# Sums of weight blocks in a seven-product FFN stage: additions on GpSimd replaced by accumulating SBUF-to-SBUF transfers in place, with the minus signs moved to the sums of x^T

## The chip, the cores and the metric

The kernel runs on one core of a Trainium2 chip. The metric is the device time of one execution in microseconds (us), as the median of several runs. The core has a matrix engine (TensorE, PE in the profile, with PEld for its weight loads), VectorE (DVE), ScalarE (ACT), GpSimd (POOL) and a sync engine (SP). Each of them works through its own queue of instructions in order. 16 DMA engines move data; transfers are issued here by SP (all weight loads) and by POOL.

## The reference, cut to what matters

The layer has two feed-forward networks, one at each end, with a recurrent branch and an attention branch between them. Only the two networks are touched by the change:

```
def swiglu(x, w1, w3, w2):
    return (jax.nn.silu(x @ w1) * (x @ w3)) @ w2
...
f = swiglu(rms_norm(h, ffn1_pre_g[l]), ffn1_w1[l], ffn1_w3[l], ffn1_w2[l])
...
f = swiglu(rms_norm(h, ffn2_pre_g[l]), ffn2_w1[l], ffn2_w3[l], ffn2_w2[l])
```

x is 512 x 1024, w1 and w3 are 1024 x 2816, all in float32. The other inputs do not matter here.

## The kernel before

**Arithmetic.** Every float32 operand of TensorE is split in two fp32r parts: `hi` is a copy of the source on ACT (it rounds), `lo` is the source minus `hi` on DVE (`split2`, lines 190 and 191). A product takes three matmuls: hi x hi, lo x hi, hi x lo.

**Units.** The first column tiles of w1 and w3 are worked one by one. A unit is a product of one 128-column tile of the weights with all of x: 24 matmuls of 512 columns (`mm_feat`, lines 200 to 202). `get` (line 159 on) loads the raw tile (`raw_...`, 512 KB, by SP, line 140) and splits it two units ahead (lines 155 and 156). There are six such tiles of w1 and of w3 in the first network (`NC1 = 6`) and four in the second (`NC2 = 4`).

**Pairs.** The remaining tiles are worked two at a time (`class Pairs`): 16 jobs in the first network, 18 in the second. A job takes two raw tiles, `ra` and `rb`, whose halves are the four blocks a11, a12 (of `ra`) and a21, a22 (of `rb`), and multiplies them with the four quarters of x^T by a scheme with seven products instead of eight. For it, sums of weight blocks (s1 to s4) and sums of the quarters of x^T (t1 to t4, function `sums`) are needed. One product is 12 matmuls of 256 columns (`mm_s`, lines 451 to 453). In job n the products stand on PE in this order: a11, s1, then a22 of the job before (`last`), then s2, a12, s4, s3. The product s2 adds onto the PSUM bank of a11, so it also waits until ACT has copied that bank out (`q1`, line 528).

**Preparation of a job.** `prep(m, i)` prepares job m in five steps. Step 0 makes the four sums with four additions of 128x512 (lines 496 to 499) into two slots of their own; POOL does them, except for the very first job, where DVE does. Steps 1 to 4 split `ra`, the slot of s1 and s2, the slot of s3 and s4, and a22. In job n, step 0 of job n+2 and steps 1 to 4 of job n+1 are issued, and `raws(n + 3)` issues the two loads of job n+3. Before the first job there are no products of pairs to hang the steps on, so they are put at points between the last units with `later`; a point comes twice in a unit, and the n-th point counts from where `later` is called. The first network has 8 units there, so `end` is 16 points.

**Slots.** All tiles of this size share 42 slots of SBUF (`NSLOT`). An instruction that writes a slot first waits until the last use of its former tile is over. This holds for SP's loads, too.

**Other work near the start.** A table of attention biases, `bias_scr`, is written to DRAM by one large transfer that POOL issues (line 672).

Of the kernel before, what the change touches and what calls it, by code (L numbers as in the profile page):

```python
# [12 lines left out]
AF = mybir.ActivationFunctionType  # L13
ALU = mybir.AluOpType

P = 128
# [35 lines left out]
def hybrid_layer(ctx: ExitStack, tc: tile.TileContext, a: dict, out: bass.AP):  # L52
    nc = tc.nc
    act, dve, pool, pe, sp = nc.scalar, nc.vector, nc.gpsimd, nc.tensor, nc.sync
# [77 lines left out]
    raws, pairs = {}, {}  # L132
# [41 lines left out]
    def later(n, fn, rank=1):  # L174
        uid[0] += 1
        due.append((now[0] + n, rank, uid[0], fn))
# [11 lines left out]
    def split2(hi, lo, src):  # L188

        act.activation(hi, src, AF.Copy)  # L190
        dve.tensor_tensor(out=lo, in0=src, in1=f32(hi), op=ALU.subtract)  # L191
# [247 lines left out]

    QH = 4 * P

    def mm_s(wa, x, ps, more=False):
# [11 lines left out]
    class Pairs:  # L456
# [13 lines left out]
        def prep(self, m, i, eng=None):  # L470
            if m >= len(self.jobs) or (m, i) in self.ready:
                return
            self.ready.add((m, i))
            k = self.k0 + 2 * m
            if i == 0:
                if k not in loaded or k + 1 not in loaded:
                    self.raws(m)
                s12, s34 = slot([P, 2 * QH], name="S12"), slot([P, 2 * QH], name="S34")
                self.w[m] = {"r": (raws.pop(k), raws.pop(k + 1)), "s": (s12, s34)}
            W = self.w[m]  # L480
            (ra, rb), (s12, s34) = W["r"], W["s"]
            a11, a12, a21, a22 = ra[:, :QH], ra[:, QH:], rb[:, :QH], rb[:, QH:]

            def both(src, w=2 * QH):
                hi = slot([P, w], F32R, name="whi")
                lo = slot([P, w], F32R, name="wlo")
                split2(hi, lo, src)
                return hi, lo

            def halves(p, a, b):  # L490
                W[a] = p[0][:, :QH], p[1][:, :QH]
                W[b] = p[0][:, QH:], p[1][:, QH:]

            if i == 0:
                e = eng or pool
                e.tensor_tensor(out=s12[:, :QH], in0=a21, in1=a22, op=ALU.add)
                e.tensor_tensor(out=s12[:, QH:], in0=s12[:, :QH], in1=a11, op=ALU.subtract)
                e.tensor_tensor(out=s34[:, QH:], in0=a12, in1=s12[:, QH:], op=ALU.subtract)
                e.tensor_tensor(out=s34[:, :QH], in0=a11, in1=a21, op=ALU.subtract)
            elif i == 1:  # L500
                halves(both(ra), "a11", "a12")
            elif i == 2:
                halves(both(s12), "s1", "s2")
            elif i == 3:
                halves(both(s34), "s3", "s4")
            elif i == 4:
                t = slot([P, 2, QH], F32R, name="w22")
                split2(t[:, 0, :], t[:, 1, :], a22)
                W["a22"] = t[:, 0, :], t[:, 1, :]
                del W["r"], W["s"]  # L510

        def run(self, tail, hooks={}):
            X = self.X
            assert st["get"] == st["split"] == self.k0, (st, self.k0)
            st["get"] = st["split"] = self.k0 + 2 * len(self.jobs)
            last = lambda: None
            for n, (nm, f) in enumerate(self.jobs):
                W = self.w.pop(n)
                first = nm == self.na
                tmp = slot([P, 4, 256], name="ct")  # L520
                q1, q5, u, v = (tmp[:, i, :] for i in range(4))
                c = slot([P, 2, SEQ], name="cc")
                if first:
                    self.c1[f] = c
                bu, bx, bc = (bank("c")[:, :256] for _ in range(3))
                at = lambda i: [f() for f in hooks.get((n, i), ())]
                mm_s(W["a11"], X["b11"], bu)
                act.activation(q1, bu, AF.Copy)
                at(1)
                mm_s(W["s1"], X["t1"], bx)  # L530
                act.activation(q5, bx, AF.Copy)
                at(2)
                last()
                self.prep(n + 1, 1)
                mm_s(W["s2"], X["t2"], bu, True)
                del W["s1"], W["s2"]
                act.activation(u, bu, AF.Copy)
                at(3)
                if n == len(self.jobs) - 1:
                    tail()  # L540
                self.prep(n + 1, 2)

                def c11():
                    mm_s(W["a12"], X["b21"], bc)
                    del W["a11"], W["a12"]
                    dve.tensor_tensor(out=c[:, 0, :256], in0=bc, in1=q1, op=ALU.add)

                if n < len(self.jobs) - 1:
                    c11()
                mm_s(W["s4"], X["b22"], bx, True)  # L550
                dve.tensor_tensor(out=c[:, 0, 256:], in0=bx, in1=u, op=ALU.add)
                self.prep(n + 1, 3)
                mm_s(W["s3"], X["t3"], bu, True)
                del W["s3"], W["s4"]
                act.activation(v, bu, AF.Copy)
                dve.tensor_tensor(out=c[:, 1, 256:], in0=v, in1=q5, op=ALU.add)
                if n == len(self.jobs) - 1:
                    c11()
                if not first:
                    c1 = self.c1[f]  # L560
                    dve.tensor_tensor(out=c1[:, 0, :], in0=c1[:, 0, :], in1=c[:, 0, :], op=ALU.mult)
                    dve.tensor_tensor(out=c1[:, 1, 256:], in0=c1[:, 1, 256:], in1=c[:, 1, 256:], op=ALU.mult)
                self.prep(n + 1, 4)
                self.prep(n + 2, 0)
                self.raws(n + 3)

                def last(W=W, bu=bu, c=c, f=f, first=first):
                    mm_s(W.pop("a22"), X["t4"], bu, True)
                    if first:
                        act.activation(c[:, 1, :256], bu, AF.Silu)  # L570
                        act.activation(c[:, 0, :], c[:, 0, :], AF.Silu)
                        act.activation(c[:, 1, 256:], c[:, 1, 256:], AF.Silu)
                    else:
                        c1 = self.c1.pop(f)
                        dve.tensor_tensor(out=c1[:, 1, :256], in0=bu, in1=c1[:, 1, :256], op=ALU.mult)
                        self.hid.f += [c1[:, 0, :], c1[:, 1, :]]

            last()


# [40 lines left out]
    pairs_a = Pairs("w1a", "w3a", NC1, X1, hid)  # L621
# [32 lines left out]
    s4 = small(NT, "s4")  # L654
# [4 lines left out]
    r = rstd_of(s4, during=lambda q: act.activation(tiny, q, AF.Silu))  # L659
# [15 lines left out]
    for t in range(NT):  # L675
        pe.matmul(psr[:, t * P : (t + 1) * P], ones, dgs[:, t, :], start=True, stop=True)
    act.activation(Rb, psr, AF.Copy)
    pairs_a.prep(0, 1)
    hid.f += [silu_mul(ps[0], ps[1], Rb), silu_mul(ps[2], ps[3], Rb)]
    pairs_a.prep(0, 2)  # L680
    later(1, lambda: pairs_a.prep(0, 3))
    later(2, lambda: pairs_a.prep(0, 4))

# [34 lines left out]
    def sums(xf):  # L718

        t = [slot([P, 4, 256], name="T") for _ in range(4)]  # L720
        pool.tensor_tensor(out=t[2], in0=xf[1, 1], in1=xf[0, 1], op=ALU.subtract)
        dve.tensor_tensor(out=t[0], in0=xf[0, 1], in1=xf[0, 0], op=ALU.subtract)
        dve.tensor_tensor(out=t[1], in0=xf[1, 1], in1=t[0], op=ALU.subtract)
        dve.tensor_tensor(out=t[3], in0=xf[1, 0], in1=t[1], op=ALU.subtract)
        return t

    def to_slots(src):
# [24 lines left out]
    later(9, lambda: X1.update(t1=to_slots(tn[0])))  # L752
    later(11, lambda: X1.update(t2=to_slots(tn[1])))
    end = 2 * 2 * (NC1 - 2)
    for i, at_ in enumerate((end - 5, end - 2, end - 1)):
        later(at_, lambda i=i: pairs_a.prep(1, i))
    swiglu_units("w1a", "w3a", 2, NC1, hid, Rb)
    point(True)
# [152 lines left out]
    for t in range(NT):  # L911
        ps = bank("v")
        c = slice(t * P, (t + 1) * P)
        o = ps[:, :256]
        for k in range(KT):
            wh, wl = wv[k // 4]
            s = slice((k % 4) * 256, (k % 4 + 1) * 256)
# [191 lines left out]
    xf = {(hh, th): slot([P, 4, 256], name="xf") for hh in range(2) for th in range(2)}  # L1109
# [10 lines left out]
        later(2 + i, lambda i=i: X2.update({f"t{i + 1}": to_slots(tn[i])}))  # L1120
    pairs_b = Pairs("w1b", "w3b", NC2, X2, hid)
    end = 2 * 2 * (NC2 - 2)
    for i, at_ in enumerate((end - 7, end - 4, end - 3, end - 2, end - 1)):
        later(at_, lambda i=i: pairs_b.prep(0, i))
    later(end, lambda: pairs_b.prep(1, 0))
    swiglu_units("w1b", "w3b", 2, NC2, hid)
    point(True)
    X2["t4"] = to_uT(tn[3], 0, 1)
# [75 lines left out]
```

## Time and profile before

| what | us |
|---|---|
| median of 3 runs | 1140.14 (1140.09 to 1140.4) |
| the profiled execution | 1140.29 |
| its span in the trace | 1138.5 |
| jobs of the first network, from 74 to 235 of the span | 161 |
| jobs of the second network, from 830 to 1012 of the span | 182 |
| POOL busy in these two stretches | 106.31 and 107.96 |
| an addition of 128x512 on POOL | 1.29 to 2.28 |
| an addition of 128x512 on DVE (lines 496 to 499) | 0.68 to 0.69 |
| a `lo` of 128x1024 on DVE, beside POOL's additions | mean 1.66 (`wlo<-S`), up to 2.31 |
| the same with POOL idle | 1.22 |

The profile gives time by engine and by line, by stretch of the span, as a chain of waits that ends with the last instruction, and as a list of instructions in order of time. "Busy" of PE counts pipelined matmuls, so that it says whether PE ever stood still, and not how near it is to its peak. Starts of instructions are in us from the start of the span.

### The profile page before, as it was taken

The numbers are of one execution on the slowest core, as the hardware profiler recorded it, in microseconds if no ns is written. First come the engines' busy times: TensorE is split into PE (matmuls) and PEld (weight loads), VectorE is DVE, ScalarE is ACT, GpSimd is POOL, SyncE is SP. The second block draws the span as 40 slices with busy tenths as digits, with TensorE's granted clock in tenths as the row PEclk, the third lists the DMA queues.
The fourth block names the chain that finished last, engine by engine and source line by source line (L and its number), as shares of the span: only waits on it lengthen the run. The fifth ranks groups of instructions, "written<-read, shape, count | busy, mean of one in ns | idle before, by whom it ended". The sixth has DMA issues, their size and how long they took to land.

```text
span 1138.5 us, 17073 instructions
## 1 busy us (share of the span) xinstructions
PE 1129.9 (99%) x6691; PEld 1006.8 (88%) x6691; DVE 778.5 (68%) x1180; ACT 572.0 (50%) x1021; POOL 341.8 (30%) x259
## 2 busy tenths in 40 slices
PE   9999999999999999999999999999999999999997
PEld 7889999988889888888888888889899999998886
DVE  5997889885447746684678864667968678985313
ACT  7445555564325357844656662356445555574211
POOL 0148677500001000001555640000655567700000
PEclk9999999999999999999999999999999999999999
DMA  9943323265314311234122333532133332255101
GB/s 339 155 138 112 100 88 111 87 210 166 98 57 152 120 56 56 90 97 130 56 78 90 93 99 105 170 126 93 37 94 112 112 98 89 93 189 180 39 19 55
DMA packets 36800, 124.93 MB, mean 110 GB/s; under 512 B 4400, under 2 KB 5936, under 8 KB 36720
## 3 DMA queue, kind: packets, MB, share of 16 engines
q1 hardware_dynamic: 34128, 115.15, 30.6%
q0 software_dynamic: 2448, 8.43, 3.9%
q8 instruction: 52, 0.85, 0.3%
q10 hardware_dynamic: 144, 0.26, 0.1%
q14 instruction: 28, 0.23, 0.1%
HBM read 116.50 MB, written 7.33 MB: 109 GB/s over the span
## 4 chain that ended last, share of the span: by engine, by line
PE 94%; DMA 4%; DVE 1%; SPq 0%; ACT 0%; issue 0%; DVEq 0%; ACTq 0%
PE f L201 11%; PE f L202 11%; PE f L200 11%; PE c L453 10%; PE c L452 10%; PE c L451 10%; PE acc L219 8%; PE acc L218 8%; PE acc L220 8%; DMA raw_w1a<-in_w1a_dram 2%; PE pt L1019 1%; DMA h<-in_x_dram 1%; PE s L983 1%; PE s L982 1%; PE tr L291 1%; PE o L1035 1%
## 5 line engine op out<-in xcount | busy, mean ns | idle before, releaser
L200 PE MATMUL f<-uT,whi 128*128 128x512 f32 (+1 forms) x536 | 196.1, 366 | 0.0
L201 PE MATMUL f<-uT,wlo 128*128 128x512 f32 (+1 forms) x536 | 195.2, 364 | 0.3 <-DVE wlo L156 0.3
L202 PE MATMUL f<-uT,whi 128*128 128x512 f32 (+1 forms) x536 | 195.1, 364 | 0.0
L218 PE MATMUL acc<-whi,hT 128*128 128x512 f32 x352 | 137.1, 390 | 0.0
L219 PE MATMUL acc<-wlo,hT 128*128 128x512 f32 x352 | 137.0, 389 | 0.0
L220 PE MATMUL acc<-whi,hT 128*128 128x512 f32 x352 | 136.9, 389 | 0.0
L201 PEld LDWEIGHTS f<-uT,wlo 128*128 128x128 f32 x536 | 101.2, 189 | 16.4 <-DVE wlo L156 0.7
L191 DVE TENSOR_TENSOR wlo<-S,whi 128x1024 fp32r<-128x1024 f32 x68 | 112.8, 1659 | 4.1 <-ACT whi L190 3.8
L453 PE MATMUL c<-Xl,whi 128*128 128x256 f32 x408 | 115.5, 283 | 0.0
L453 PE MATMUL c<-uT,whi 128*128 128x256 f32 x408 | 115.5, 283 | 0.0
L452 PE MATMUL c<-Xh,wlo 128*128 128x256 f32 x408 | 115.5, 283 | 0.0
L452 PE MATMUL c<-uT,wlo 128*128 128x256 f32 x408 | 115.5, 283 | 0.0
L451 PE MATMUL c<-Xh,whi 128*128 128x256 f32 x408 | 115.5, 283 | 0.0
L451 PE MATMUL c<-uT,whi 128*128 128x256 f32 x408 | 115.5, 283 | 0.0
L202 PEld LDWEIGHTS f<-uT,whi 128*128 128x128 f32 x536 | 101.1, 189 | 15.9
L200 PEld LDWEIGHTS f<-uT,whi 128*128 128x128 f32 x536 | 101.2, 189 | 15.6
L1003 POOL TENSOR_SCALAR P<-P,d 128x256 f32<-128x256 f32 (+1 forms) x64 | 63.1, 1001 | 56.0 <-DVE d L1001 33.9
L452 PEld LDWEIGHTS c<-Xh,wlo 128*128 128x128 f32 x408 | 78.3, 192 | 0.0
L452 PEld LDWEIGHTS c<-uT,wlo 128*128 128x128 f32 x408 | 78.3, 192 | 0.0
L451 PEld LDWEIGHTS c<-Xh,whi 128*128 128x128 f32 x408 | 78.3, 192 | 0.0
L451 PEld LDWEIGHTS c<-uT,whi 128*128 128x128 f32 x408 | 78.3, 192 | 0.0
L453 PEld LDWEIGHTS c<-uT,whi 128*128 128x128 f32 x408 | 78.3, 192 | 0.0
(313 smaller groups left out, 2673.7 us busy)
## 6 DMA issues: line engine op xcount, KB each, us to landing
raw_w2a<-in_w2a_dram SPq DMA_DIRECT2D x22, 512.0 KB, 4.1
raw_w1b<-in_w1b_dram SPq DMA_DIRECT2D x22, 512.0 KB, 3.9
raw_w3b<-in_w3b_dram SPq DMA_DIRECT2D x22, 512.0 KB, 3.9
raw_w2b<-in_w2b_dram SPq DMA_DIRECT2D x22, 512.0 KB, 4.2
raw_w3a<-in_w3a_dram SPq DMA_DIRECT2D x21, 512.0 KB, 4.4
raw_w1a<-in_w1a_dram SPq DMA_DIRECT2D x20, 512.0 KB, 4.3
raw_wg<-in_wg_dram SPq DMA_DIRECT2D x16, 512.0 KB, 4.0
raw_xr<-in_xr_dram SPq DMA_DIRECT2D x8, 512.0 KB, 3.9
```

Of the source, the lines that this page charges most:

```text
L191: dve.tensor_tensor(out=lo, in0=src, in1=f32(hi), op=ALU.subtract)
L200: pe.matmul(ps[:, c0:c1], wh[:, s], h_, start=k == 0, stop=False)
L201: pe.matmul(ps[:, c0:c1], wl[:, s], h_, start=False, stop=False)
L202: pe.matmul(ps[:, c0:c1], wh[:, s], l_, start=False, stop=k == KT - 1)
L218: pe.matmul(acc[n], x[:, 0, c], wh[:, s], start=first, stop=False)
L219: pe.matmul(acc[n], x[:, 0, c], wl[:, s], start=False, stop=False)
L220: pe.matmul(acc[n], x[:, 1, c], wh[:, s], start=False, stop=last)
L291: pe.transpose(ps[:, k * P : (k + 1) * P], hg[:, kk * P : (kk + 1) * P], ident)
L451: pe.matmul(ps, wh[:, s], xh, start=first, stop=False, skip_group_check=True)
L452: pe.matmul(ps, wl[:, s], xh, start=False, stop=False, skip_group_check=True)
L453: pe.matmul(ps, wh[:, s], xl, start=False, stop=k == 3, skip_group_check=True)
L1003: pool.tensor_scalar(out=pt[:, x, b0:256], in0=pt[:, x, b0:256], scalar1=d[:, x : x + 1], scalar2=None, op0=ALU.mult)
```

## The change

The sums of a job are made in place, in the raw tiles, all with a plus sign, by four additions in this order, called A1 to A4 below:

- A1: a22 += a21 (this is s1)
- A2: a21 += a11 (s3)
- A3: a11 += a22 (s2)
- A4: a12 += a11 (s4)

On the first job of the first network DVE does them, as before. On all others each is a transfer from SBUF to SBUF with addition at the destination, issued by POOL: 128 rows of 2 KB, 256 KB. Since the blocks are overwritten, a22 and `ra` have to be split before: step 0 is now the split of a22 and A1, step 1 the split of `ra` and A2 to A4, step 2 the split of `rb` (s3 and s1), step 3 the split of `ra` again (s2 and s4). In job n, steps 0 and 1 of job n+2 and steps 2 and 3 of job n+1 are issued. A1 to A4 depend on each other: A2 reads and overwrites a21 after A1 has read it, A3 adds what A1 left in a22 to the a11 that A2 has read, and A4 adds what A3 left. In the program each of A2 to A4 waits on POOL for the landing of the one before it; A1 waits for its raw tile and for the split of a22, A3 also for the split of `ra`.

Two slots per job for s1 to s4 are no longer taken. Ahead of the first job, the steps stand at other points. The signs that the sums of the weights lose are given to t1 to t4 (DVE makes all four now; one was POOL's before) and to three reads of PSUM: two copies on ACT with scale -1, an addition turned into a subtraction, and a multiplication on DVE with a scalar of -1 added. The program has the same 6,686 matmuls; POOL's additions of two tensors go from 150 to 16, and its transfers from 28 to 160.

```
             if i == 0:
                 if k not in loaded or k + 1 not in loaded:
                     self.raws(m)
-                s12, s34 = slot([P, 2 * QH], name="S12"), slot([P, 2 * QH], name="S34")
-                self.w[m] = {"r": (raws.pop(k), raws.pop(k + 1)), "s": (s12, s34)}
+                self.w[m] = {"r": (raws.pop(k), raws.pop(k + 1))}
...
+            def add(to, x):
+                if eng:
+                    eng.tensor_tensor(out=to, in0=to, in1=x, op=ALU.add)
+                else:
+                    pool.dma_start(out=to, in_=x, accum_op=ALU.add)
...
             if i == 0:
-                e = eng or pool
-                e.tensor_tensor(out=s12[:, :QH], in0=a21, in1=a22, op=ALU.add)
-                e.tensor_tensor(out=s12[:, QH:], in0=s12[:, :QH], in1=a11, op=ALU.subtract)
-                e.tensor_tensor(out=s34[:, QH:], in0=a12, in1=s12[:, QH:], op=ALU.subtract)
-                e.tensor_tensor(out=s34[:, :QH], in0=a11, in1=a21, op=ALU.subtract)
-            elif i == 1:
-                halves(both(ra), "a11", "a12")
-            elif i == 2:
-                halves(both(s12), "s1", "s2")
-            elif i == 3:
-                halves(both(s34), "s3", "s4")
-            elif i == 4:
                 t = slot([P, 2, QH], F32R, name="w22")
                 split2(t[:, 0, :], t[:, 1, :], a22)
                 W["a22"] = t[:, 0, :], t[:, 1, :]
-                del W["r"], W["s"]
+                add(a22, a21)
+            elif i == 1:
+                halves(both(ra), "a11", "a12")
+                add(a21, a11)
+                add(a11, a22)
+                add(a12, a11)
+            elif i == 2:
+                halves(both(rb), "s3", "s1")
+            elif i == 3:
+                halves(both(ra), "s2", "s4")
+                del W["r"]
...
                 act.activation(q5, bx, AF.Copy)
                 at(2)
+                self.prep(n + 2, 0)
                 last()
-                self.prep(n + 1, 1)
+                self.prep(n + 2, 1)
                 mm_s(W["s2"], X["t2"], bu, True)
...
-                self.prep(n + 1, 2)
+                self.raws(n + 3)
...
                 dve.tensor_tensor(out=c[:, 0, 256:], in0=bx, in1=u, op=ALU.add)
-                self.prep(n + 1, 3)
+                self.prep(n + 1, 2)
                 mm_s(W["s3"], X["t3"], bu, True)
                 del W["s3"], W["s4"]
-                act.activation(v, bu, AF.Copy)
-                dve.tensor_tensor(out=c[:, 1, 256:], in0=v, in1=q5, op=ALU.add)
+                act.activation(v, bu, AF.Copy, scale=-1.0)
+                dve.tensor_tensor(out=c[:, 1, 256:], in0=v, in1=q5, op=ALU.subtract)
...
-                self.prep(n + 1, 4)
-                self.prep(n + 2, 0)
-                self.raws(n + 3)
+                self.prep(n + 1, 3)
...
-    pairs_a.prep(0, 1)
+    pairs_a.prep(0, 1, dve)
     hid.f += [silu_mul(ps[0], ps[1], Rb), silu_mul(ps[2], ps[3], Rb)]
-    pairs_a.prep(0, 2)
-    later(1, lambda: pairs_a.prep(0, 3))
-    later(2, lambda: pairs_a.prep(0, 4))
+    later(1, lambda: pairs_a.prep(0, 2))
+    later(2, lambda: pairs_a.prep(0, 3))
...
-        pool.tensor_tensor(out=t[2], in0=xf[1, 1], in1=xf[0, 1], op=ALU.subtract)
-        dve.tensor_tensor(out=t[0], in0=xf[0, 1], in1=xf[0, 0], op=ALU.subtract)
-        dve.tensor_tensor(out=t[1], in0=xf[1, 1], in1=t[0], op=ALU.subtract)
-        dve.tensor_tensor(out=t[3], in0=xf[1, 0], in1=t[1], op=ALU.subtract)
+        dve.tensor_tensor(out=t[0], in0=xf[0, 0], in1=xf[0, 1], op=ALU.subtract)
+        dve.scalar_tensor_tensor(out=t[1], in0=xf[1, 1], scalar=-1.0, in1=t[0], op0=ALU.mult, op1=ALU.subtract)
+        dve.tensor_tensor(out=t[2], in0=xf[1, 1], in1=xf[0, 1], op=ALU.subtract)
+        dve.scalar_tensor_tensor(out=t[3], in0=t[1], scalar=-1.0, in1=xf[1, 0], op0=ALU.mult, op1=ALU.subtract)
...
-    for i, at_ in enumerate((end - 5, end - 2, end - 1)):
+    for i, at_ in enumerate((end - 9, end - 8, end - 2, end - 1)):
         later(at_, lambda i=i: pairs_a.prep(1, i))
...
-    for i, at_ in enumerate((end - 7, end - 4, end - 3, end - 2, end - 1)):
-        later(at_, lambda i=i: pairs_b.prep(0, i))
-    later(end, lambda: pairs_b.prep(1, 0))
+    for m, i, at_ in ((0, 0, end - 7), (0, 1, end - 6), (1, 0, end - 5), (1, 1, end - 4), (0, 2, end - 2), (0, 3, end - 1)):
+        later(at_, lambda m=m, i=i: pairs_b.prep(m, i))
```

More of the change, by code (lines that the diff above doesn't have):

```diff
@@ L477, in prep @@
                     self.raws(m)
-                s12, s34 = slot([P, 2 * QH], name="S12"), slot([P, 2 * QH], name="S34")
-                self.w[m] = {"r": (raws.pop(k), raws.pop(k + 1)), "s": (s12, s34)}
+                self.w[m] = {"r": (raws.pop(k), raws.pop(k + 1))}
             W = self.w[m]
-            (ra, rb), (s12, s34) = W["r"], W["s"]
+            ra, rb = W["r"]
             a11, a12, a21, a22 = ra[:, :QH], ra[:, QH:], rb[:, :QH], rb[:, QH:]
@@ L569, in last @@
                     if first:
-                        act.activation(c[:, 1, :256], bu, AF.Silu)
+                        act.activation(c[:, 1, :256], bu, AF.Silu, scale=-1.0)
                         act.activation(c[:, 0, :], c[:, 0, :], AF.Silu)
@@ L574, in last @@
                         c1 = self.c1.pop(f)
-                        dve.tensor_tensor(out=c1[:, 1, :256], in0=bu, in1=c1[:, 1, :256], op=ALU.mult)
+                        dve.scalar_tensor_tensor(out=c1[:, 1, :256], in0=bu, scalar=-1.0, in1=c1[:, 1, :256], op0=ALU.mult, op1=ALU.mult)
                         self.hid.f += [c1[:, 0, :], c1[:, 1, :]]
```

## The prediction

> **What bounds the kernel now.** I read the share of each engine first, then the chain of waits, then stretches of the span.
>
> ```profile
> PE 1129.9 (99%) x6691; PEld 1006.8 (88%) x6691; DVE 778.5 (68%) x1180; ACT 572.0 (50%) x1021; POOL 341.8 (30%) x259
> PE 94%; DMA 4%; DVE 1%; SPq 0%; ACT 0%; issue 0%; DVEq 0%; ACTq 0%
> 0.00:20.00 20.00, 18.55 (x71) 14.59 (x72) 12.06 (x24) 13.37 (x25) 2.04 (x9) 1.00 0.91 306
> 40.00:60.00 20.00, 19.73 (x88) 16.00 (x87) 19.83 (x30) 5.73 (x7) 2.40 (x1) 1.00 0.99 152
> 74.00:235.00 161.00, 161.00 (x1344) 161.00 (x1343) 133.81 (x138) 90.99 (x158) 106.31 (x56) 1.00 0.35 115
> 830.00:1012.00 182.00, 182.00 (x1516) 181.92 (x1515) 141.89 (x152) 99.71 (x174) 107.96 (x63) 1.00 0.33 105
> ```
>
> The last four rows are stretches: from and to, length, then busy time of PE, PEld, DVE, ACT and POOL, PE's clock, the share of the DMA engines, GB/s. In both stretches of pairs PE never stands still, at full clock: 161 us for 1,344 matmuls is 0.12 us each, whatever DVE and POOL do beside it. A product is 12 x 0.12 = 1.44 us and a job seven of them, 10.08 us (ACT's copy of `q1`, line 528, also returns every 10.08 us). PE's idle time is 1138.5 - 1129.9 = 8.6 us, most of it in the tail; before 80 us it is 1.45 + 0.27 = 1.7 us. So whatever the change frees on POOL and DVE has at most 1.7 us to win. It can only lose, if a sum comes too late.
>
> **POOL's additions removed.** 132 of them go, some 1.3 to 2.3 us each. They lay beside PE. DVE's `lo` gets shorter with them (1.66 to 1.22 us), also beside PE. Worth: 0. The scale of -1 and the fourth sum of x^T on DVE (1.22 us at 128x1024) cost about what DVE saves near the start, where POOL's sum had stretched line 414 to 1.80 us from 0.69: 0.
>
> **The chain of transfers.** A2, A3 and A4 each wait on POOL for the landing of the one before, and POOL's queue is in order, so A1 of the next job stands behind A4 of this one; only A4's landing and the next A1 overlap. If a transfer takes L from issue until a waiting instruction runs, and P is POOL's own time to issue one, jobs can leave POOL no faster than every 3L + P. POOL's transfers in the trace:
>
> ```profile
> L964 POOL DMA_DIRECT2D BT<-bias_scr x16: 536/536/590, 523.9 to 607.5; - x16
> DMA to landing us min/median/max: 2.3/2.4/4.1
> DMA to landing us min/median/max: 3.9/4.7/7.3
> 523.89 2.17 POOL L964 DMA_DIRECT2D BT<-bias_scr  x4 [164.81 <-PE f L202]
> 527.99 0.30 POOL L965 MEMSET BT<- 64x256 f32 x1 [1.92 <-DMA BT<-bias_scr]
> 528.61 2.12 POOL L964 DMA_DIRECT2D BT<-bias_scr  x4
> 533.89 0.31 POOL L965 MEMSET BT<- 64x256 f32 x1 [3.17 <-DMA BT<-bias_scr]
> ```
>
> The first two lines are BT, 128 KB each: P = 0.54, landing 2.4. The third is the loads of line 248, 512 KB each: 3.9 at best. The rest is POOL in order of time: the fourth BT transfer starts at 523.89 + 2.17 - 0.54 = 525.52 and the memset that waits for it at 527.99, so L = 2.47. In the second group, with a weight load issued at 529.07 beside it, it is 533.89 - 530.19 = 3.70: 1.2 us more.
>
> No row shows a transfer that adds. Lower bound: it costs what a copy of 256 KB would, between the two rows, 2.4 + (3.9 - 2.4) x 128/384 = 2.9. Upper bound: it reads source and destination, so it costs as 512 KB do, 3.9, plus, with SP's two loads in each job, 1.2 us on two of three transfers, 0.8 each: 4.7. Below a plain copy nothing can lie. I take the middle of 2.9 and 3.9 with one such meeting in most jobs: 3.4 + 0.3 = 3.7. POOL's period is then 3 x 3.7 + 0.54 = 11.64, 1.56 above the job's 10.08. It decides from 3L + P = 10.08, L = 3.18.
>
> The lead that hides the first jobs: A1 of job n+2 can be issued 2.88 (two products) + 0.38 (`q5`) + 0.62 + 0.68 (split of a22) = 4.6 us into job n. A4 is wanted 2.0 us into job n+2: s2 is its fourth product, at 4.32, less 1.05 + 1.22 for the split. That is 2 x 10.08 + 2.0 - 4.6 = 17.6 us for 4L = 14.8; slack 2.8. Second network, jobs 2 to 17: 15 periods x 1.56 = 23.4, less the slack 2.8, plus 1.7 because job 0's chain starts only some 17 us ahead and pushes the next two: **22**. First network, jobs 2 to 15: 13 x 1.56 = **20**, with no slack left after the start below. ACT and DVE wait in order, too: behind the late second split of `ra` stand `q1` and the split of a22 for two jobs on, but both are needed later than s2 is, so they add nothing.
>
> **The start.** Step 0 of job 1 moves from POOL at point 11 to ACT and DVE at point 7. Job 1's raw tiles aren't there then:
>
> ```profile
> 51.43 6.00 SPq L140 DMA_DIRECT2D raw_w3a<-in_w3a_dram  x2
> 51.74 1.04 ACT L190 ACTIVATE Xh<-xn 128x1024 fp32r<-128x1024 f32 x1
> 54.26 1.06 ACT L155 ACTIVATE whi<-raw_w1a 128x1024 fp32r<-128x1024 f32 x1 [1.48 <-DMA raw_w1a<-in_w1a_dram]
> 65.74 1.29 POOL L496 TENSOR_TENSOR S<-raw_w3a 128x512 f32<-128x512 f32 x1 [13.57 <-DMA raw_w3a<-in_w3a_dram]
> bias_scr<-erow POOLq DMA_DIRECT2D x1, 3064.0 KB, 33.6
> ```
>
> SP issues them at 51.43 and 57.1; POOL, which had nothing else to do, waited 13.57 us for them, until 65.74, because `bias_scr` filled the DMA engines until 29.6 + 33.6 = 63.2. In the changed program the split of a22 stands on ACT right after `Xh<-xn` (51.74), and behind it the split of `ra` and then `whi` of the seventh of eight units (54.26 now). ACT would wait there, and DVE with it. SP can issue these loads some 5 to 10 us earlier in the changed program (fewer slots are taken; the second one waits for the third unit's end, about 47), but they stand in SP's queue behind the eighth unit's tile, which landed at 32.7 + 28.2 = 60.9. So they land between 60.9 and 65.1; I take T = 63. Then a22 (0.62 on ACT), `ra` (1.05) and the unit's split (1.05 + 1.22, with DVE's hand-over) put its `lo` at T + 4 = 67, and PE wants it at 30.3 + 6 x 5.46 = 63.1 (units take 24 x 0.2275 us, the first of the eight starts at 30.3): **3.9**.
>
> The chain of job 1 starts at T + 1.4 and ends at T + 1.4 + 4L; the second split of `ra` waits for it on ACT, and behind it stand a `silu` and `q1` of job 0. With 2.3 for the split and 2.8 for those, `q1` is done at T + 4L + 6.5; s2 of job 0 wants it at T + 4 + 2 x 5.46 + 2.88 = T + 17.8. So 4L - 11.3 = **3.5** at L = 3.7.
>
> Sum: 22 + 20 + 3.9 + 3.5 = 49.4, on the span of 1138.5. The profiled execution took 1140.29, 1.8 more than its span and 0.15 more than the median, so 1138.5 + 49.4 + 1.8 = 1189.7: I say **1190**.
>
> The Trainium skill, "DMA: Bandwidth & Descriptors" (Anatomy of one DMA — SWDGE (gpsimd) path), gives about 2.0 us plus bytes/436e3 for a transfer that POOL issues, and "Collectives: The Full Stack" (The bandwidth ceiling) says that a reducing transfer is slower than a copy because it needs two source reads, not because of the add. As an estimate from the two, 2.0 + 524/436 = 3.2 alone; the BT row agrees with the first (2.3 by it, 2.4 measured); no run here shows the second. By them the period would be 10.1, next to the job's 10.08, and the sum about 1146.
>
> **The rivals.** (1) *The chain fits under a job.* A transfer from SBUF to SBUF that costs as a plain copy, L = 2.9, gives 3 x 2.9 + 0.54 = 9.24, under 10.08. For it: BT's 2.4. Against: the destination is read too, and loads take a third of the DMA engines (0.35 and 0.33 above). Left is the start, 3.9 + 0.3: 1140.3 + 4.2 = 1144.5; the skill's formula above lies at its edge. (2) *Adding is slow in itself.* If the adder passes data slower than 512 KB would go, L = 6: period 18.5, excess 8.5; 13 x 8.5 + 15 x 8.5 + 17 at the start = 255: 1395. For and against: no row. (3) *Not slower.* Job 1's raw tiles land early enough, before 63.1 - 4.0 = 59.1, and L is under 2.83, which hides both prices of the start; then only DVE's relief is left, up to 1.7 us: 1139. For it: SP's loads wait less for slots. Against: the tile ahead of them in SP's queue landed at 60.9. That the program doesn't do what it says I rule out: its list of instructions has 132 transfers in place of the additions.
>
> **How the numbers follow.** No change that a measurement of this kernel can tell is within 0.2%, 2.3 us. Chances: forecast (L 3.2 to 4.7) 0.55, rival 1 0.25, rival 2 0.10, rival 3 0.10. The forecast's own ends: L = 3.2 gives about 1147; L = 4.7 a period of 14.64, excess 4.56: 59 + 4 and 68 + 6 in the two networks, 3.9 + 7.5 at the start, 1289. The range takes in rival 1 but for its lowest part: 1143 to 1285; outside are rival 2 and most of rival 3. Faster by over 0.2% would need more than PE's 1.7 us: 0.02; within 0.2%: 0.09, rival 3 and rival 1 with tiles that land at 60.9 (1.8 + 0.3); slower: 0.89.
>
> **What would show it.** Gaps of PE before s2 (lines 451 to 453) that end with a `lo` of line 191, which waited for a transfer of POOL; POOL's transfers evenly 3L + 0.54 per job; PE busy in the pairs' stretches below their length. If PE stays gapless there, L is under 3.2 and rival 1 holds. At the start, ACT should idle from about 53 until job 1's raw tile lands, and PE before the seventh unit. Wrong altogether I'd be if the transfers land in under 2.8 us and the stretch from 0 to 74 keeps its length.

## The result, and the profile after

| | before | after |
|---|---|---|
| median, us | 1140.47 (1140.09 to 1140.76, 6 runs) | 1307.61 (1304.7 to 1312.33, 6 runs) |
| the profiled execution, its span | 1140.29, 1138.5 | 1304.7, 1302.7 |

The ratio is 1.147 (95% interval 1.1459 to 1.1482): 14.7% slower. The forecast of 1190 had the side right and the size wrong, and the time lies above the range's upper end of 1285.

The share of each engine and the chain of waits of the changed kernel:

```profile
PE 1191.7 (91%) x6691; PEld 1054.3 (81%) x6691; DVE 698.8 (54%) x1182; ACT 569.4 (44%) x1021; POOL 212.4 (16%) x257
PE 58%; DMA 21%; issue 9%; POOL 3%; DVE 1%; ACT 1%; POOLq 0%; DVEq 0%; ACTq 0%
```

PE stands still for 1302.7 - 1191.7 = 111.0 us, against 8.6 before, and a fifth of the chain that sets the end is now DMA. PE's busy time also grew, by 61.8 us for the same matmuls. The two stretches of pairs (from and to, length, busy time of PE, PEld, DVE, ACT, POOL, PE's clock, share of the DMA engines, GB/s) and PE's longest waits (us in all, times, longest) show where:

```profile
84.00:315.00 231.00, 189.18 (x1344) 183.41 (x1343) 99.28 (x139) 90.10 (x159) 48.60 (x56) 0.87 0.61 140
908.00:1173.00 265.00, 211.72 (x1499) 204.15 (x1498) 105.14 (x147) 96.40 (x171) 58.19 (x67) 0.87 0.60 132
```

```profile
PE c L452 <- ACT ct L533: 77.0, 20, 7.8
PE c L453 <- DVE wlo L191: 14.8, 29, 0.9
PE f L200 <- ACT whi L155: 4.7, 1, 4.7
```

The 1,344 matmuls that took 161 us take 231 now, at a mean granted clock of 0.87. PE waits before s2 for `q1` (line 533 here, 528 before), 77.0 us in all. ACT makes `q1` late because it stands in ACT's queue behind the second split of `ra`, which waits for a transfer. In order of time, one job of POOL's transfers and what is beside it:

```profile
136.48 0.87 SPq L140 DMA_DIRECT2D raw_w3a<-in_w3a_dram  x2
136.65 1.21 POOL L498 DMA_DIRECT2D raw_w3a<-raw_w3a  x1
142.26 1.06 ACT L190 ACTIVATE whi<-raw_w1a 128x1024 fp32r<-128x1024 f32 x1 [5.39 <-DMA raw_w1a<-raw_w1a]
144.97 0.86 POOL L498 DMA_DIRECT2D raw_w3a<-raw_w3a  x1 [7.11 <-DMA raw_w3a<-raw_w3a]
148.72 0.86 POOL L498 DMA_DIRECT2D raw_w3a<-raw_w3a  x1 [2.88 <-DMA raw_w3a<-raw_w3a]
152.20 0.86 POOL L498 DMA_DIRECT2D raw_w3a<-raw_w3a  x1 [2.62 <-DMA raw_w3a<-raw_w3a]
```

The four POOL rows are A1 to A4 of one job. From A3 to A4 it takes 152.20 - 148.72 = 3.48 us, with nothing beside it; from A2 to A3 3.75. But from A1 to A2 it takes 8.32: A4 of the job before was still under way (ACT gets it only at 142.26), and SP had issued two loads of 512 KB 0.17 us earlier. A1 of the next job is issued 0.54 us after A4 (a row at 152.74), so POOL is not out of work between jobs. From the last job back, A4 returns every (300.55 - 104.16)/13 = 15.11 us in the first network and every (1161.18 - 919.99)/16 = 15.07 in the second; the forecast was 11.64.

The start shows both waits that the prediction named:

```profile
66.47 0.63 ACT L190 ACTIVATE w<-raw_w3a 128x512 fp32r<-128x512 f32 x1 [12.35 <-DMA raw_w3a<-in_w3a_dram]
69.04 0.80 PE L200 MATMUL f<-uT,whi 128*128 128x512 f32 x1 [4.69 <-ACT whi L155]
```

ACT stands for 12.35 us before job 1's raw tile, PE then 4.69 us before the seventh unit, and the first product of a pair starts at 83.15 instead of 73.79, 9.4 us later. The first matmul that needs this unit's `lo` starts at 70.49 instead of 63.13, which is 7.4 us. The other 2.0 come from the matmuls behind it: they take 0.43 us each in place of 0.23 up to 74.5, at a mean granted clock of 0.54 from 69 to 75.

The traces also give a lag: the start of a matmul less the start of the same one, counted in program order, in the kernel before. It is 9.4 us at the first product of a pair, 12.9 behind s2 of job 0, 78.9 at the end of the first network and 163.7 at the end of the second.

My theory from these rows: the landings that POOL's queue waits out one after the other set the period of a job (the chain), and its 15.1 us are made of the transfers alone, their adding, and the loads beside them. The rivals: the traffic as such, PE's lowered clock, and the new order of the steps.

### The profile page after: what moved, and what is told of

It reads as the page before. It is cut to its first block, busy times and chain, and to the rows that moved or that the text cites. A ratio compares the mean times of both kernels' runs of the same rounds, so it can differ in the third digit from the quotient of the medians.

```text
span 1302.7 us, 17240 instructions
## 1 busy us (share of the span) xinstructions
PE 1191.7 (91%) x6691; PEld 1054.3 (81%) x6691; DVE 698.8 (54%) x1182; ACT 569.4 (44%) x1021; POOL 212.4 (16%) x257
## 4 chain that ended last, share of the span: by engine, by line
PE 58%; DMA 21%; issue 9%; POOL 3%; DVE 1%; ACT 1%; POOLq 0%; DVEq 0%; ACTq 0%
PE f L200 9%; PE f L201 9%; PE f L202 9%; PE acc L220 7%; PE acc L219 7%; PE acc L218 7%; DMA raw_w3b<-raw_w3b 7%; DMA raw_w1b<-raw_w1b 6%; DMA raw_w1a<-raw_w1a 4%; DMA raw_w3a<-raw_w3a 4%; PE c L453 2%; PE c L454 2%; PE c L452 2%; PE pt L1022 1%; POOL raw_w3b L498 1%
## 5 line engine op out<-in xcount | busy, mean ns | idle before, releaser
L452 PE MATMUL c<-Xh,whi 128*128 128x256 f32 x408 | 128.6, 315 | 80.2 <-ACT ct L533 77.0
L452 PEld LDWEIGHTS c<-Xh,whi 128*128 128x128 f32 x408 | 87.6, 215 | 85.2 <-ACT ct L533 81.7
L453 PE MATMUL c<-Xh,wlo 128*128 128x256 f32 x408 | 130.1, 319 | 14.9 <-DVE wlo L191 14.8
L454 PE MATMUL c<-Xl,whi 128*128 128x256 f32 x408 | 125.5, 307 | 0.0
L452 PE MATMUL c<-uT,whi 128*128 128x256 f32 x408 | 125.2, 307 | 0.0
L454 PE MATMUL c<-uT,whi 128*128 128x256 f32 x408 | 123.6, 303 | 0.0
L453 PEld LDWEIGHTS c<-Xh,wlo 128*128 128x128 f32 x408 | 87.8, 215 | 22.9 <-DVE wlo L191 22.7
L452 PEld LDWEIGHTS c<-uT,whi 128*128 128x128 f32 x408 | 89.2, 219 | 0.0
L454 PEld LDWEIGHTS c<-Xl,whi 128*128 128x128 f32 x408 | 88.8, 218 | 0.0
L453 PEld LDWEIGHTS c<-uT,wlo 128*128 128x128 f32 x408 | 88.4, 217 | 0.0
L454 PEld LDWEIGHTS c<-uT,whi 128*128 128x128 f32 x408 | 87.7, 215 | 0.0
L219 PEld LDWEIGHTS acc<-wlo,hT 128*128 128x128 f32 x352 | 66.1, 188 | 13.7
```

What stands on the lines that cost most here:

```text
L219: pe.matmul(acc[n], x[:, 0, c], wl[:, s], start=False, stop=False)
L452: pe.matmul(ps, wh[:, s], xh, start=first, stop=False, skip_group_check=True)
L453: pe.matmul(ps, wl[:, s], xh, start=False, stop=False, skip_group_check=True)
L454: pe.matmul(ps, wh[:, s], xl, start=False, stop=k == 3, skip_group_check=True)
```

## The experiments

The time of the kernel before beside these runs was 1140.39 to 1140.76. Runs without an interval are single ones. Line 498 is the transfer, and L499 or L504 where an edit moves it.

**No dependence between the transfers.**

```
-                    pool.dma_start(out=to, in_=x, accum_op=ALU.add)
+                    pool.dma_start(out=to, in_=f32(uT[:, 0, 7, :]), accum_op=ALU.add)
```

> All 132 transfers stay, with the same bytes and the same adding, but each adds one fixed tile of x^T instead of another block of the pair, so that A2, A3 and A4 no longer wait for the landing of the transfer before (the sums hold other data). Chain theory (the wait of each transfer for the one before, in POOL's order, sets a job's time): POOL issues A2 to A4 at once, PE is gapless again in the stretches of pairs, and only the start's price is left: 1140 + 8 to 15 = 1148 to 1155. Rival (the transfers' traffic itself, or the sharing of DMA engines or SBUF, holds the kernel up): the time stays near 1305, at least above 1250.

Measured: 1150.02. In the middle of the first network's pairs, a stretch of this run:

```profile
85.00:235.00 150.00, 150.00 (x1252) 150.00 (x1252) 89.78 (x126) 81.21 (x141) 49.07 (x56) 1.00 0.85 200
```

PE is gapless at full clock, although the DMA engines are busier (0.85) than in the changed kernel (0.61). The same transfers, bytes and adding cost nothing when nobody on POOL waits for a landing. This shows the chain, and rules out the traffic as such. The 9.4 us left are the start's: its first product of a pair stands at 83.16, and the lag is 9.37 there and to the last matmul. Of these 9.4, 5.8 are longer waits of PE (3.64, 1.63 and 0.78 less 0.27), and 3.6 the growth of its busy time (1133.5 against 1129.9), at a granted clock of 0.50 from 69 to 75 us.

**The same sums in place by POOL, without transfers.**

```
-                    pool.dma_start(out=to, in_=x, accum_op=ALU.add)
+                    pool.tensor_tensor(out=to, in0=to, in1=x, op=ALU.add)
```

> The same four sums in the same order, in place and at the same points, but as additions on POOL (1.3 to 2.3 us each in the profile of before) instead of transfers. Chain theory: four additions of some 2 us are 8 us a job, under its 10.08, so PE is gapless in the pairs and only the start's price stays: 1145 to 1152. Rival (the order of the steps, or the sums of x^T and the scales of -1 that came with them, cost the time): near 1305.

Measured: 1156.25, 4 above the upper end expected and far from the rival. PE idles 1154.5 - 1136.4 = 18.1 us, 8.9 of them at the start (waits of 4.6 and 4.3 us at lines 200 and 201, whose units come before the pairs). The lag is 11.6 us at the first product of a pair and grows by another 4.4 in the two networks' pairs, where none was expected. The order of the steps and the moved signs are not what costs 167 us.

**No loads beside the chain.**

```
+        if k in reused:
+            loaded.add(k)
...
-                self.w[m] = {"r": (raws.pop(k), raws.pop(k + 1))}
+                self.kept[m] = self.kept.pop(m - 3) if m > 2 else (raws.pop(k), raws.pop(k + 1))
+                self.w[m] = {"r": self.kept[m]}
```

> From the fourth job of each network on, the raw tiles of three jobs before are used again and nothing is loaded for them (the sums pile up on old data; about 29 of 36 jobs' loads are left out). Chain with loads beside it (SP's two 512 KB loads of each job stretch one or two of its transfers to 6 to 9 us, from 3.5 to 4.4 without): the period of POOL's chain falls from 15.1 to about 4.4 + 3.7 + 3.5 + 0.5 = 12.1 us, 3 us less for about 28 jobs: 1305 - 84 = about 1220, in 1205 to 1240. Rival (a transfer takes its 4.85 us on average whatever is beside it): 1295 to 1310.

Measured: 1232.79; A4 returns every 12.95 and 12.84 us in the two networks, in place of 15.1. POOL's rows in order of time:

```profile
168.56 1.22 POOL L504 DMA_DIRECT2D raw_w1a<-raw_w1a  x1
172.91 0.86 POOL L504 DMA_DIRECT2D raw_w1a<-raw_w1a  x1 [3.13 <-DMA raw_w1a<-raw_w1a]
176.59 0.86 POOL L504 DMA_DIRECT2D raw_w1a<-raw_w1a  x1 [2.83 <-DMA raw_w1a<-raw_w1a]
180.18 1.75 POOL L504 DMA_DIRECT2D raw_w1a<-raw_w1a  x2 [2.72 <-DMA raw_w1a<-raw_w1a]
186.22 0.86 POOL L504 DMA_DIRECT2D raw_w1a<-raw_w1a  x1 [4.29 <-DMA raw_w1a<-raw_w1a]
```

The first four rows are a bare job: 4.35 with A4 of the job before under way, 3.68, 3.59, and 0.54 to the next A1 (the row with x2 is A4 and A1). Its shortest form, 4.36 + 3.70 + 3.47 + 0.54 = 12.07, comes back to a few hundredths all through the run. So the loads cost 15.1 - 12.9 = 2.2 us a job, and a bare job is still above 10.08. Some 0.8 us a job is left over: about every third job has one transfer that is 1 to 2 us longer, as the one from the A1 in the fourth row to the last row is (186.22 - 180.72 = 5.5).

**Copies in place of additions.**

```
-                    pool.dma_start(out=to, in_=x, accum_op=ALU.add)
+                    pool.dma_start(out=to, in_=x)
```

> The same chain of transfers with plain copies instead of transfers that add (the sums are left out, the copied block stands in their place). Chain theory with adding as a second read of the destination: a copy has half the reads, so it takes between 2.9 and 3.5 alone against 3.5, and the period falls from 15.1 by 0 to 2.5 us: 1230 to 1305. Rival (adding is slow in itself, and a copy would fit under a job): period below 10.08, 1145 to 1160. Rival (the adding costs nothing; fixed latency and meetings with loads are all): 1300 to 1310.

Measured: 1187.36, between the ranges, with periods of 11.22 and 11.93 us. Adding costs more than I had allowed. The first line below is from this run's list by line (duration on POOL, min/median/max in ns, first and last start in us), the second the same of the changed kernel:

```profile
L498 POOL DMA_DIRECT2D raw_w1b<-raw_w1b x36: 536/536/541, 831.9 to 1033.3; - x36
```

```profile
L498 POOL DMA_DIRECT2D raw_w1b<-raw_w1b x36: 855/862/1212, 888.5 to 1149.0; - x36
```

A transfer that adds takes POOL 0.86 us to issue, a copy 0.54. From A3 to A4 the shortest is 2.49 for copies and 3.45 for additions: 0.96 more, 0.32 of it on POOL. The rest is on the DMA engines. What they moved in windows of 4 us, so 0.1 us a number, first where one transfer that adds was under way (the run without loads), then where a copy was (the run with both cuts, below; at its edges the copies before and after it):

```profile
GB/s 0 0 0 0 0 0 0 0 0 0 0 0 0 0 0 0 0 0 0 164 205 225 205 164 266 225 164 225 225 184 205 164 0 0 0 0 0 0 0 0
```

```profile
GB/s 287 0 0 0 0 0 0 0 0 0 0 41 492 410 369 492 451 328 41 0 0 0 0 0 0 0 0 0 0 0 0 0 0 0 0 0 0 410 492 369
```

The addition moves its 256 KB in 1.3 us at some 200 GB/s, the copy in about 0.65 us at some 430. Adding halves the rate: 0.65 + 0.32 = 0.97 us.

**PE kept busy in its waits.**

```
+            idle = bank("w")
...
+                for _ in range(32):
+                    pe.matmul(idle[:, :256], W["a11"][0][:, :P], X["b11"](0, 0), start=True, stop=True)
                 mm_s(W["s2"], X["t2"], bu, True)
```

> 32 matmuls that nobody reads stand before s2 of each job, some 3.8 us in PE's idle time there (a job's own matmuls are 10.1 of the 15.1 us). If the chain on POOL sets the period and PE's lowered clock (0.76 to 0.98 in the pairs) lies inside PE's waits: the granted clock rises toward 1.0, the time stays at 1300 to 1315. Rival (the lowered clock is a cost of its own, the 61.8 us that PE's busy time grew by): the kernel gets faster by 20 to 60 us, 1245 to 1285.

Measured: 1302.25, with 34 x 32 = 1,088 more matmuls. The stretches of pairs:

```profile
84.00:315.00 231.00, 228.04 (x1868) 226.51 (x1867) 101.59 (x142) 92.82 (x161) 48.48 (x56) 0.99 0.62 146
908.00:1173.00 265.00, 255.95 (x2083) 253.24 (x2082) 107.76 (x150) 98.33 (x174) 58.06 (x67) 0.99 0.60 134
```

The clock is back at 0.99 and the time is the same. So PE's slower matmuls in the pairs cost nothing: they fill time in which PE would have waited.

**The early steps of job 1 later.**

```
-    for i, at_ in enumerate((end - 9, end - 8, end - 2, end - 1)):
+    for i, at_ in enumerate((end - 4, end - 3)):
```

> The first two steps of job 1 of the first network move to three and four units before the end of the units, where job 1's raw tiles have landed (steps 2 and 3 fall to job 0's own points). If the split of a22 that waits for the raw tile on ACT is the start's price: the waits of 12.35 us on ACT and of 4.7 us on PE before 85 us are gone, the first pair's product starts near 74 to 76 instead of 84, but job 1's chain starts later; with POOL's period of 15.1 behind it the total falls by 0 to 10 us, 1295 to 1305. Rival (it is the chain of job 1 itself that keeps the start late): no earlier first product.

Measured: 1302.95. The first product of a pair starts at 75.01, 8.1 us earlier than in the changed kernel, and the whole wins 4.7 on its median (1.75 on the profiled execution). Both predicted waits at the start are gone, and most of what they cost comes back as waits for the chain, which runs on at 14.95 and 15.17 us a job.

**An eighth of the bytes.**

```
-                    pool.dma_start(out=to, in_=x, accum_op=ALU.add)
+                    pool.dma_start(out=to[:, :64], in_=x[:, :64], accum_op=ALU.add)
```

> Each transfer takes only 64 of its 512 columns, 32 KB instead of 256 KB (the other 448 columns of each sum are left out); chain, issue and order stay. If most of a transfer is a fixed time (the 128 KB copies of before took 2.47): 2.0 to 2.4 us each, period 6.5 to 8, under a job, and the time is 1145 to 1160. If what is slow is to stand beside SP's 512 KB loads, however short the transfer: period above 10, 1170 to 1260.

Measured: 1182.36, periods 11.32 and 11.21. This is the second case. In order of time:

```profile
133.77 0.86 POOL L498 DMA_DIRECT2D raw_w3a<-raw_w3a  x1 [1.58 <-DMA raw_w3a<-raw_w3a]
134.31 1.21 POOL L498 DMA_DIRECT2D raw_w1a<-raw_w1a  x1
137.08 0.86 POOL L498 DMA_DIRECT2D raw_w1a<-raw_w1a  x1 [1.55 <-DMA raw_w1a<-raw_w1a]
137.87 1.67 SPq L140 DMA_DIRECT2D raw_w1a<-in_w1a_dram  x2
142.92 0.86 POOL L498 DMA_DIRECT2D raw_w1a<-raw_w1a  x1 [4.98 <-DVE w L191]
```

Alone a transfer of 32 KB takes 2.44 us (the row at 133.77 has its forerunner at 131.33), and 137.08 - 134.31 = 2.77 behind another. Beside SP's two loads it takes 142.92 - 137.08 = 5.84, some 3 us more, though it has only an eighth of the bytes to move. (The last row names a split on DVE, which ended at the same time; the transfer of 137.08 itself lands 5.3 us after its issue.) Other long ones of this run stand beside loads in the same way (4.91 at 112.01 with loads at 112.66, 6.08 at 148.71 with loads at 148.17). Over the whole run, the 36 transfers A2 to A4 that were under way beside neither a load nor a packet of the instruction queue (more on these at the end) landed in 2.12 to 2.19 us; of the 56 beside a load, 29 took over 2.6, up to 6.7. Per job, the period is 2.8 us above the bare one (11.3 against 2.77 + 2.69 + 2.45 + 0.54 = 8.45), as it is 3.0 above with 256 KB (15.1 against 12.07). So meeting the loads costs a time of its own, which hardly depends on the transfer's bytes.

**One of the four by POOL.**

```
-            def add(to, x):
+            def add(to, x, eng=eng):
...
-                add(a21, a11)
+                add(a21, a11, eng or pool)
```

> A2 (a21 += a11) is done by POOL in place, the other three stay transfers, so POOL waits for the landing of A1 before A2 (as now), then goes on without a landing between A2 and A3, and waits for A3 before A4: per job two landings and one addition instead of three landings. Chain theory: the period falls from 15.1 to about 6.0 + 1.9 + 4.0 + 0.5 = 12.4, 2.7 us less for some 30 jobs: 1305 - 80 = 1225, in 1205 to 1250. Rival (the count of transfers or bytes decides, a quarter less): 1264, a quarter of the 164 us off.

Measured: 1220.5, periods 12.08 and 12.84: near the chain theory's 1225, and not the 1264 of a quarter less traffic. What counts is how many landings POOL waits out.

**Copies and no loads.** The edits of both runs together.

> Both cuts at once: plain copies instead of transfers that add, and no loads from the fourth job of each network on (sums and most loads are left out). By the terms measured so far the three parts of POOL's period add up: copies alone 2.75 + 2.75 + 2.5 + 0.53 = 8.5 us and no meetings with loads, which is under a job's 10.08; so PE is gapless in the pairs and only the start's price stays: 1145 to 1158, against 1187 with copies alone and 1233 without loads alone. Rival (the two cuts work on the same time, so that the second adds little): 1175 to 1187.

Measured: 1150.71. Its stretches of pairs:

```profile
84.00:235.00 151.00, 151.00 (x1261) 151.00 (x1260) 90.84 (x127) 81.94 (x141) 30.04 (x56) 1.00 0.29 112
861.00:1012.00 151.00, 151.00 (x1261) 151.00 (x1260) 88.96 (x127) 79.89 (x140) 30.58 (x57) 1.00 0.28 108
```

With both parts gone a period can be as short as 8.5 us, under a job, and the chain is hidden as the first rival of the prediction had it. What is left is the start's: the lag is 9.9 us at the first product of a pair and 10.0 at the last matmul. Either part alone lifts it above 10.08: 11.2 to 11.9 with loads, 12.9 with adding.

**In place on POOL, with the later start.** The edits of the second and the sixth experiment together.

> The sums in place by additions on POOL, and the first two steps of job 1 of the first network at three and four units before the end. If the 16 us that the additions on POOL still cost with the early steps all lie at the start (ACT's wait for the raw tile of job 1, and the chain of job 1 behind it): 1139 to 1143. Rival (some of it lies in the pairs, where DVE waits for POOL or shares with it): 1146 to 1156.

Measured: 1148.07, ratio to before 1.0067 (1.0053 to 1.0082). The later start wins 8.2 of the 15.9 us. The 7.7 that stay are the rival's case: some of the cost lies in the pairs. PE's waits (us, times, longest):

```profile
PE c L453 <- DVE wlo L191: 2.3, 3, 1.6
PE f L201 <- DVE wlo L156: 1.6, 1, 1.6
PE w L606 <- DVE tiny L610: 1.4, 1, 1.4
```

The first two were 0 and 0.27 us before. The lag is 1.6 us at the first product of a pair, 5.7 at the end of the first network and 8.0 at the end of the second. So 1.6 us lie at the start and 6.4 in the pairs. Only part of these are waits: from 160 to 200 us PE is busy throughout in both kernels, yet it has 332 matmuls there against 335 before. The two runs in which the chain doesn't hold PE up (no dependence; copies without loads) have the same order of steps and their lag doesn't grow in the pairs, so this goes with the additions on POOL. How they slow PE was not taken apart.

**Two chains side by side.** A3 and A4 of a job are issued one job later, each just before A1 and A2 of the next; with the later start.

```
+            if i == 0 and rest:
+                rest.pop(0)()
...
-                add(a21, a11)
-                add(a11, a22)
-                add(a12, a11)
+                if rest:
+                    rest.pop(0)()
+                add(a21, a11)
+                rest += [lambda: add(a11, a22), lambda: add(a12, a11)]
+                while rest and (eng or m in (0, len(self.jobs) - 1)):
+                    rest.pop(0)()
```

> The same 132 transfers that add, with the same bytes and dependences, the early steps as late as in the run of that name, and another order on POOL: A3 and A4 of a job are issued one job later, each just before A1 and A2 of the next one, so that two chains of two are under way side by side. Chain theory (what costs is the landings that POOL's queue waits out one after the other, three a job): some two landings in the order of 4.4 us a job and 1 to 3 us of meetings with loads, 8 to 11 us against a job's 10.08: 1142 to 1180. Rival (the number of adding transfers beside the loads sets the time, in whatever order): above 1260.

Measured: 1203.51, ratio to before 1.053 (1.0491 to 1.057). It lies between the ranges: 99 us better than the version with the later start alone, 24 above my upper end. In order of time:

```profile
105.10 0.86 POOL L499 DMA_DIRECT2D raw_w3a<-raw_w3a  x1 [6.94 <-DVE wlo L191]
105.64 1.21 POOL L499 DMA_DIRECT2D raw_w1a<-raw_w1a  x1
108.60 0.86 POOL L499 DMA_DIRECT2D raw_w3a<-raw_w3a  x1 [1.75 <-DMA raw_w3a<-raw_w3a]
109.98 0.86 POOL L499 DMA_DIRECT2D raw_w1a<-raw_w1a  x1 [0.53 <-DMA raw_w1a<-raw_w1a]
110.33 0.83 SPq L140 DMA_DIRECT2D raw_w1a<-in_w1a_dram  x2
```

The first round (A3 and A1, then A4 and A2) takes 109.98 - 105.10 = 4.9 us. Then SP's loads come, and the next A3, which waits for the landing of this A2, leaves POOL only at 116.98: 7.0 us. Two landings in place of three, and the meeting with the loads stays: 12 us a job there. In a stretch of the second network A1 returns every 10.1 us (952.46 to 1002.90 in five rounds), and there the chain keeps up with PE.

**Halves.**

```
-                    pool.dma_start(out=to, in_=x, accum_op=ALU.add)
+                    for c in (slice(0, 256), slice(256, 512)):
+                        pool.dma_start(out=to[:, c], in_=x[:, c], accum_op=ALU.add)
```

> Each transfer is cut into two of 256 columns each, 128 KB, issued one after the other; the chain is the same. If the fixed part (2.4 us at 32 KB) and the meetings with loads rule: a half alone takes 2.9, its sister lands 0.5 to 0.9 later, three waits a job are 3 x 2.9 + two more issues + 3 of meetings = 13 to 15 us, 1230 to 1305. Rival (bytes rule, and halves overlap fully): 11 to 12 us, 1170 to 1200.

Measured: 1280.56, in the range expected; the last transfer of a job returns every 14.36 us in the first network and 14.48 in the second. Cutting each transfer in two wins 27 of the 167 us: the chain is as many landings long as before.

## Why the prediction was wrong in size

**What bounds the kernel, and the freed work.** Right. DVE's busy time fell by 80 us and POOL's by 129, and nothing of it was won: in the run without dependence the two are as low (698.9 and 213.4 us) and PE is gapless in the pairs, and the lag stays at 9.37 us from the first product to the last.

**The chain of transfers.** The mechanism was right: transfers waited out one after the other on POOL hold back s2. PE's waits there end with `q1` (77.0 us) and only in small part with a `lo` (14.8), which the prediction named as the sign, but both stand behind the same late split. The step that failed is the length of the chain's links: "I take the middle of 2.9 and 3.9 with one such meeting in most jobs: 3.4 + 0.3 = 3.7". By its parts, for a job:

| part of POOL's period, us | forecast | measured |
|---|---|---|
| three transfers alone | 3 x 3.4 = 10.2 | 3 x 3.47 = 10.4 |
| A1 while A4 is still under way; A2 to A3 | 0 | 0.9 + 0.2 |
| from A4 to A1 | 0.54 | 0.54 |
| meeting SP's loads | 3 x 0.3 = 0.9 | 2.2 |
| longer ones without loads | 0 | 0.8 |
| sum | 11.64 | 15.1 |

The middle of the bounds was good for a transfer alone (3.47 against 3.4), in part by luck: a plain copy takes 2.49 and not the 2.9 of the lower bound, and adding 0.96 on top of it, a third of that on POOL. What was wrong is everything that it meets. I took A1's overlap with A4 as free; it costs 0.9. And I priced a meeting with SP's loads from one row, 1.2 us for BT beside one load, once or less in a job. Every job issues two loads together, and the run with 32 KB shows some 3 us where they meet a transfer. The upper bound, 4.7 a transfer, was short for the same reason: (15.1 - 0.54)/3 = 4.85. An excess of 5.03 in 13 periods and of 4.99 in 16 is 65 + 80 = 145 us, where 20 + 22 stood. The lag gives all terms of the sum:

| term, us | forecast | measured |
|---|---|---|
| start, up to the first product of a pair | 3.9 | 9.4 |
| s2 of job 0 | 3.5 | 3.6 |
| the rest of the first network | 20 | 66.0 |
| second network | 22 | 84.7 |
| sum | 49.4 | 163.7 |

**P.** The issue of a transfer that adds takes 0.86 us, and not BT's 0.54. A1 may start 0.54 after A4, but it then lasts 1.21: the two take 1.75, as the row with x2 in the run without loads shows, which is two full issues. So P was some 0.3 us too small; in the table above this is a part of the 0.9 that A1 loses beside A4.

**The start.** Right in kind. The raw tile landed at 66.4 in place of 63 (I had bounds of 60.9 and 65.1), which turns the forecast's 3.9 into 7.3, and 7.4 is what PE lost up to the first matmul with that `lo`. The other 2.0 of the 9.4, from slower matmuls behind the wait, were not forecast. The 3.5 before s2 of job 0 came out at 3.6, but only 1.8 of it is waiting and the rest slower matmuls, so the agreement is in part luck. Once the chain is slower than PE, the start is no cost of its own: taking it away wins 2 to 5 us, since PE then waits longer for the chain.

**The rivals.** The first, that the chain fits under a job, is what happens with copies and without loads; with only one of the two it does not. The second, that adding is slow in itself, has a part of the truth: adding halves the rate and takes POOL 0.32 us more, some 0.97 us a transfer over a copy, where its L of 6 supposed 3.1 over the copy's 2.9. The third, not slower, needed job 1's raw tiles before 59.1 (they landed at 66.4) and an L under 2.83 (3.47 alone).

**The rule that I weighed.** The Trainium skill, "DMA: Bandwidth & Descriptors" (Anatomy of one DMA — SWDGE (gpsimd) path) and "Collectives: The Full Stack" (The bandwidth ceiling), gave 3.2 us as an estimate for a transfer alone. The runs agree: 2.49 for a copy of 256 KB (2.6 by the formula) and 3.45 for an addition, within 0.1 of the 3.2 and the 0.32 us more on POOL. That adding needs two source reads agrees with the 200 against 430 GB/s. The estimate failed as a forecast because it holds for a transfer alone.

**What a clock below 1 is worth.** I had not foreseen that PE's clock would fall with its gaps. "TensorE: Matmul & The Clock Gate" (Part 1: The HAM clock gate) of the Trainium skill says that an idle stretch throttles the clock and sustained work releases it; 0.87 in the pairs with gaps and 0.99 with the 32 matmuls in them agree. In the pairs the growth of PE's busy time is an effect of the waits and no cost beside them. It is a cost where PE itself sets the pace behind a wait: 3.6 of the 9.4 us that the run without dependence loses at its start.

## What to carry to other kernels

Price a chain of dependent transfers by the time from issue to issue in the stretch where it will run, with the loads that run there, and not by a transfer alone: here 3.5 us became 4.85. When a queue in order waits out the landings, their number per job counts: one landing fewer won 87 us and two chains side by side 99 over the same start, while moving only an eighth of the bytes, which leaves most of each sum undone, won 125 and still did not bring the chain under a job. A busy time that grows at a lower clock is a cost only if that engine sets the pace, which a little idle work in its gaps can show.

## What the runs showed of the hardware that was not expected

- A transfer that adds, SBUF to SBUF, 256 KB: 3.45 us from issue to the dependent issue (a copy 2.49, an addition of 32 KB 2.41), with 0.86 us of POOL in place of 0.54 and some 200 GB/s in place of 430.
- A small transfer is no safer beside large loads than a large one: 32 KB took 5.84 us beside two loads of 512 KB. The Trainium skill, "DMA: Bandwidth & Descriptors" (Queues, rings and completion order), says, where it treats transfers that SP and ACT issue, that the semaphore write of a transfer lands only after every earlier write of that DMA engine, across its queues. If this holds for POOL's transfers too, a short one would wait for the loads' writes, as seen here; no run tells it apart from other ways of sharing an engine.
- Transfers that were 1 to 2 us longer with no load beside them (the run without loads) stood beside a single packet of the instruction queue, which moved at some 16 GB/s. Four long ones of four had such a packet, four ordinary ones none. The whole trace of that run bears it out: the 62 transfers A2 to A4 that were under way beside neither a load nor such a packet landed in 3.15 to 3.25 us, and of the 29 beside a packet alone, 11 took over 3.65, up to 5.4. This is seen side by side only; no run took the packets away.
